# A two-layer hybrid block: transposes and some norms taken from TensorE to block transposes on VectorE and small DMAs

## The chip, the cores and the metric

The kernel runs on one core of a Trainium2 chip. A core has five engines with queues of their own: TensorE (PE in the profile; its weight loads are PEld), VectorE (DVE), ScalarE (ACT), GpSimd (POOL) and SyncE (SP), which here does nothing but issue DMAs. TensorE writes its results to PSUM, from where VectorE or ScalarE read them. The metric is device microseconds of one execution; the time of a kernel is the median of its runs.

## The reference, cut to what matters

All arithmetic is float32: 1024 tokens, width 1024, two layers. Layer 0 mixes by retention (4 heads) and by a gated delta rule (4 heads), layer 1 by a gated linear recurrence; a convolutional feed-forward follows each.

```
def _rms(x):
    return xf * lax.rsqrt(jnp.mean(xf * xf, axis=-1, keepdims=True) + EPS)

for layer in range(DEPTH):
    hn = rms_norm(h, norm_mix[layer])
    h = h + (retention_deltanet_mixer if layer % 2 == 0 else rglru_mixer)(hn, ...)
    h = h + conv_ffn(rms_norm(h, norm_ffn[layer]), ...)
return rms_norm(h, norm_final)

# retention, chunks of 128
scores = einsum('bhnid,bhnjd->bhnij', qc, kc) * dmask
intra  = einsum('bhnij,bhnjv->bhniv', scores, vc)
kv     = einsum('bhncd,bhncv->nbhdv', k_tail, vc)      # state: s = s * chunk_decay + kv_n
inter  = einsum('bhncd,nbhdv->bhncv', q_decay, s_prev)

# gated delta rule, per chunk (q and k are l2-normalised, (lmat + I) solved for u and w)
v_new = u_n - einsum('bhcd,bhdv->bhcv', w_n, s)
o = einsum('bhcd,bhdv->bhcv', qd_n, s) + einsum('bhij,bhjv->bhiv', a_n, v_new)
s = s * cd_n + einsum('bhcd,bhcv->bhdv', kt_n, v_new)
```

## The kernel before, in words

Activations are kept transposed, channels on the 128 partitions and tokens along the free axis: the residual is `H`, eight tiles of 128 x 1024. A weight matrix is streamed in quarters of 128 x 512. SP loads a quarter into `raw`, ScalarE makes its rounded part `whi` (L270), VectorE the rest `wlo` (L271), and each product is three matmuls (L328 to L330: high by high, high by low, low by high). The ring of split quarters holds six; `prefetch` keeps the loads ahead of use. A slot is one such triple over 512 tokens. `project` (L364) does one output tile of 128 channels in two halves of 512 tokens, eight slots each, and evacuates each half, multiplying by `R`, the row of inverse norms of the tokens, copied to all partitions (L388).

Small work is woven between these slots. `slot` counts them; `after(n, f)` emits `f` n slots later, and a lane is a list of generators of which one step is emitted every second slot. What is emitted is then ordered on each engine by a planner that estimates when each instruction could start; only in places marked `manual_schedule` is the written order kept.

`_mix0` is the first stage, some 470 us. In order: projections of the delta rule's k heads, q heads, gates of retention (`gate2`), v heads; meanwhile the lane `gdn` makes each chunk's matrix (`a_stage`), inverts its 32 x 32 blocks on VectorE by 31 substitution steps (L1271, L1273) by way of `l_dram` and `t_dram`, and merges them (`merge`, L1305 to L1339). Then, during the twelve projections of retention (per head q, k, v), the lane `gdn` runs the `scan` over eight chunks and the lane `ret` runs `ret_half` twice per head. Last come the gates of the delta rule and `_mix0_out`.

Things that need the other orientation go through TensorE: a transpose is a product with the identity. `scan` transposes v (L1389) and k (L1397) of a chunk, `ret_half` transposes v (L1459) and k (L1464) of four chunks, and `normalise` transposes its output eight slots later (L1366), from where ScalarE copies it and SP stores it in `y_dram`. Sums over channels, that is over partitions, are products with a column of ones: the q heads' norms (`qnorm`, L1345) and the norms of tokens (`norm_tok`, L433), whose result, inverse square roots on POOL (L438), is spread over the partitions by a product with the identity (`norm_row`, L448). `square_step` gathers the squares of eight tiles in one accumulator, but for the last tile, which is an accumulator of its own. In the scan a chunk's state product K by S (L1404), its four vector updates (L1406), L by v (L1410), the state's update (L1417, L1422) and the output (L1427, L1428) are separate lane steps. Retention's states lie in two places, used in turn, and are updated chunk by chunk between the output products (L1478, L1483).

Norms are needed in nine places of 512 or 256 tokens: the start (two halves, `norm_rest`), the two mixers' outputs (`down_pairs`, two halves each, followed by `pair_operands`, which builds the feed-forward's operands), layer 0's feed-forward output (`down_x`, two halves) and the end (`final`: 512, 256 and 256).

In the feed-forward the down product works on seven operands per set of eight pairs. `hidden` and `store_parts` store them in DRAM: operands 0, 1, 3 and 5 as two halves each (`pf_dram`, high and low), 2, 4 and 6 as one (`sf_dram`), split by ScalarE and VectorE (L840, L841) when `load_set` brings them back.

Of the kernel before, what the change touches and what calls it, by code (L numbers as in the profile page):

```python
# [19 lines left out]
P = 128  # L20
T = 1024
# [82 lines left out]
class Block:  # L104
    def __init__(self, ctx, tc, I, out, stop=None):
# [35 lines left out]
        pad(self.sm, 40, "pad3")  # L141
        self.nhalo = 0
        self.npp = 0
        self.lo_engine = nc.vector
# [42 lines left out]
    def quarter_order(self):  # L187
# [3 lines left out]
        for h in range(NH):  # L191
            o += [(("mix_in", i), 2) for i in (h, 4 + h, 8 + h)]
# [209 lines left out]
    def square_step(self, st, k, src, w=HALF):  # L402
# [14 lines left out]
        if k == KT - 1:  # L417
            st["acc"].append(sq)
        else:
            nc.vector.tensor_tensor(st["acc"][0], st["acc"][0], sq, ALU.add)  # L420

# [136 lines left out]
    def pair_operands(self, st, n, gain, gap):  # L558
# [13 lines left out]
        yield from self.norm_tok(st, wait=2)  # L572
# [3 lines left out]
        yield from range(gap)  # L576
        self.run(self.norm_row(st, apart=True))
        rows = st["rows"]
# [181 lines left out]
    def ffn(self, layer, gain):  # L760
# [3 lines left out]
        s_dram = self.tc.dram_tile([2, 4, 4, P, HALF], F32, name=f"sf_dram{layer}")  # L764
# [15 lines left out]
        place = {1: 0, 4: 1, 2: 2, 6: 3}  # L780
        whole = {0: 0, 1: 1, 3: 2, 5: 3}
        room = {}

        def store_parts(p, y, hi):
# [11 lines left out]
            def store_split(o, src, at):  # L796
                A.copy(halves(hi[:, at]), src)  # L797
                V.tensor_tensor(halves(lo[:, at]), src, f32(halves(hi[:, at])), ALU.subtract)
                for e, t in enumerate((hi, lo)):
                    nc.sync.dma_start(p_dram[c, whole[o], k % 4, e], f32(t[:, at]))  # L800
# [22 lines left out]
            store_split(5, v[:, :, 0], slice(HALF, T))  # L823

        def load_set(c, o):

            x = self.operand(o)
            if o in whole:
                for k in range(4):
                    for e in range(2):  # L830
                        nc.sync.dma_start(f32(x[:, :, 4 * e + k, :]), halves(p_dram[c, whole[o], k, e]))
# [74 lines left out]
    def final(self, ys, name):  # L906
# [13 lines left out]
        def part(t0, w, left):  # L920

            sl = slice(t0, t0 + w)
            st = {}
# [13 lines left out]
        s1 = part(512, 256, {2: [lambda: run(self.norm_tok(s0[0]))], 6: [lambda: run(self.norm_row(s0[0], 0))]})  # L937
# [14 lines left out]
    def rglru(self, gain):  # L952
# [5 lines left out]

        sm = lambda name: pool.tile([P, 8], F32, name=name)
# [12 lines left out]
        us = pool.tile([P, 8 * HALF], F32, name="us")  # L972
        xs = pool.tile([P, 4 * T], F32R, name="xs")
# [110 lines left out]
    def mix0(self, gain):  # L1084
        tc = self.tc
        self.q_dram = tc.dram_tile([NCH, P, HALF], F32, name="q_dram")
        self.v_dram = tc.dram_tile([NCH, P, HALF], F32, name="v_dram")
# [21 lines left out]
    def _mix0(self, room):  # L1109
# [89 lines left out]
        def conv_tail(kind, h, buf, dst):  # L1199
# [9 lines left out]
            return th  # L1209

# [131 lines left out]
        def qnorm(h, s):  # L1342
            p = self.pc()
            for n in range(NCH):
                PE.matmul(p[:, n:n + 1], s[:, n * P:(n + 1) * P], self.ones, start=True, stop=True)  # L1345

            V.tensor_scalar(irho[:, h * NCH:(h + 1) * NCH], p[:, 0:NCH], 4.0 * EPS, 128.0 * EPS, ALU.add, ALU.mult)

        def normalise(o, eps, ydst, i):
# [13 lines left out]
            def post():  # L1363
                p = self.pc()
                for h in range(4):
                    PE.transpose(p[:, hs(h)], on[:, hs(h)], self.ident)  # L1366
                A.copy(s, p)
                nc.sync.dma_start(ydst, ps4(s) if len(ydst.shape) == 3 else s)
            self.after(8, post)

        def scan(n):
# [4 lines left out]
            nc.sync.dma_start(v, self.v_dram[n])  # L1376
# [10 lines left out]
            pv = self.pc()  # L1387
            for h in range(NH):
                PE.transpose(pv[:, hs(h)], v[:, hs(h)], self.ident)  # L1389
# [319 lines left out]
```

## Time and profile before

| | us |
|---|---|
| median of 3 runs (2198.58 to 2200.04) | 2199.09 |
| the profiled execution | 2200.31 |
| span of its trace, first to last instruction | 2198.5 |
| PE busy | 2176.4 |
| DVE busy | 1696.0 |
| ACT busy | 1069.7 |
| POOL busy | 80.8 |

The granted TensorE clock is 0.998 over the span. Busy times of PE are of overlapping instructions, so the mean of one is longer than the time by which it moves the next; that is read from the starts in the timeline. In a row of a group the numbers after the bar are busy us, mean ns of one, and the engine's idle time before them with what ended it. In a row of waits they are us in total, times, and the longest.

### The profile page before, as it was taken

To read this page: it belongs to the slowest core of one execution; us is meant where nothing else is said; L and a number is where in the kernel's file an instruction comes from. 1 tells how busy PE (TensorE), PEld (TensorE's weight loads), DVE (VectorE), ACT (ScalarE), POOL (GpSimd) and SP (SyncE) were. 2 spreads that over 40 slices of the span, in tenths; PEclk is the share of its full clock that TensorE was granted. 3 is DMA by queue.
4 is the path that set the end of the run, shared out by engine and by line. 5 is a ranking of instruction groups with operands and counts; after the bars stand their busy time and mean duration, and the time that the engine had idled before them with its cause. 6 is when DMAs were issued, how large, how long until landed. Compare 5 with 4: busy or idle time off the path is not lost.

```text
span 2198.5 us, 29909 instructions
## 1 busy us (share of the span) xinstructions
PE 2176.4 (99%) x10844; PEld 1819.5 (83%) x10844; DVE 1696.0 (77%) x2576; ACT 1069.7 (49%) x1712; POOL 80.8 (4%) x73
## 2 busy tenths in 40 slices
PE   9999999999999999999999999999999999999998
PEld 8887888887888888887888888888888888878888
DVE  6988766446899988987865677778999889878644
ACT  5334433124565555554323476765655555544321
POOL 0100111200000000000000000000000000000001
PEclk9999999999999999999999999999999999999999
DMA  4243424125234544438546211242245445375542
GB/s 173 81 141 99 128 83 145 57 79 175 63 120 167 179 153 157 163 111 287 197 160 201 82 53 63 85 147 73 101 165 171 148 173 177 115 271 178 190 165 77
DMA packets 203300, 305.34 MB, mean 139 GB/s; under 512 B 31728, under 2 KB 91408, under 8 KB 203152
## 3 DMA queue, kind: packets, MB, share of 16 engines
q1 hardware_dynamic: 202720, 301.85, 40.7%
q8 instruction: 85, 1.39, 0.3%
q10 hardware_dynamic: 432, 1.58, 0.2%
q14 instruction: 63, 0.52, 0.1%
HBM read 212.63 MB, written 90.72 MB: 138 GB/s over the span
## 4 chain that ended last, share of the span: by engine, by line
PE 89%; DMA 4%; DVE 4%; issue 2%; ACT 1%; POOL 1%; SPq 0%; POOLq 0%; DVEq 0%; ACTq 0%
PE ps L328 27%; PE ps L330 27%; PE ps L329 27%; DMA t<-sf_dram 1%; DMA t<-y_dram 1%; PE pc L433 1%; DMA s<-pf_dram 1%; DMA h<-in_xT_dram 0%; DVE wlo L271 0%; PE pc L448 0%; DVE l L1273 0%; DVE l L1271 0%; PE pc L328 0%; PE pc L330 0%; PE pc L329 0%
## 5 line engine op out<-in xcount | busy, mean ns | idle before, releaser
L328 PE MATMUL ps<-s,whi 128*128 128x512 f32 (+1 forms) x2792 | 1091.0, 392 | 3.9 <-ACT s L840 1.8
L329 PE MATMUL ps<-s,whi 128*128 128x512 f32 (+1 forms) x2792 | 1084.5, 388 | 1.0 <-DVE s L841 0.7
L330 PE MATMUL ps<-s,wlo 128*128 128x512 f32 (+1 forms) x2792 | 1083.9, 388 | 0.0
L270 ACT CAST whi<-raw 128x512 fp32r<-128x512 f32 (+1 forms) x612 | 371.5, 613 | 659.1 <-PE ps L329 515.6
L328 PEld LDWEIGHTS ps<-s,whi 128*128 128x128 f32 x2792 | 524.9, 188 | 112.5 <-ACT s L840 3.1
L330 PEld LDWEIGHTS ps<-s,wlo 128*128 128x128 f32 x2792 | 524.7, 188 | 108.1 <-DVE wlo L271 0.3
L329 PEld LDWEIGHTS ps<-s,whi 128*128 128x128 f32 x2792 | 525.2, 188 | 107.3 <-DVE s L841 1.8
L271 DVE TENSOR_TENSOR wlo<-raw,whi 128x512 fp32r<-128x512 f32 (+1 forms) x612 | 412.9, 680 | 60.8 <-ACT whi L270 57.2
L774 DVE SCALAR_TENSOR_TENSOR t<-halo,cols,t 128x1024 f32<-128x1024 f32 x176 | 222.1, 1282 | 4.8 <-ACT t L772 3.5
L747 DVE TENSOR_TENSOR halo<-ps,kept 128x512 f32<-128x512 f32 (+1 forms) x138 | 92.2, 668 | 75.5 <-PE ps L330 74.2
L757 DVE TENSOR_TENSOR h<-ps,h 128x512 f32<-128x512 f32 x112 | 77.4, 691 | 82.2 <-PE ps L330 81.9
L772 ACT ACTIVATE t<-halo,cols 128x1024 f32<-128x1024 f32 x88 | 109.7, 1246 | 16.9 <-DVE halo L747 11.6
L742 ACT COPY kept<-ps 128x512 f32<-128x512 f32 (+1 forms) x138 | 77.0, 558 | 13.3 <-PE ps L330 11.2
L498 DVE TENSOR_TENSOR h<-ps,h 128x512 f32<-128x512 f32 (+1 forms) x72 | 45.3, 631 | 43.3 <-PE ps L330 43.3
L438 POOL TENSOR_TENSOR rtok<-rtok,npow 128x4 f32<-128x4 f32 (+1 forms) x11 | 11.2, 1016 | 1722.3 <-DVE rtok L437 1668.7
L857 DVE TENSOR_TENSOR t<-t 128x1024 f32<-128x1024 f32 x44 | 53.7, 1221 | 0.0
L797 ACT CAST t<-t 128x512 fp32r<-128x512 f32 x64 | 38.1, 620 | 32.0 <-DVE t L857 30.7
L852 ACT ACTIVATE t<-t 128x1024 f32<-128x1024 f32 x44 | 46.8, 1063 | 10.1 <-DVE t L774 10.0
L416 ACT ACTIVATE t<-h 128x512 f32<-128x512 f32 (+1 forms) x49 | 27.2, 562 | 46.3 <-DVE h L498 41.5
L840 ACT CAST s<-t 128x512 fp32r<-128x512 f32 x48 | 29.5, 621 | 38.4 <-DMA t<-sf_dram 34.0
L328 PE MATMUL ps<-s,s 128*128 128x256 f32 (+1 forms) x144 | 46.2, 321 | 0.0
L329 PE MATMUL ps<-s,s 128*128 128x256 f32 (+1 forms) x144 | 45.8, 318 | 0.0
(293 smaller groups left out, 2074.5 us busy)
## 6 DMA issues: line engine op xcount, KB each, us to landing
raw<-in_ffn_up_dram SPq DMA_DIRECT2D x176, 256.0 KB, 2.7
s<-pf_dram SPq DMA_DIRECT2D x128, 256.0 KB, 5.3
pf_dram<-t SPq DMA_DIRECT2D x64, 256.0 KB, 2.6
pf_dram<-lo SPq DMA_DIRECT2D x64, 256.0 KB, 2.5
sf_dram<-t SPq DMA_DIRECT2D x64, 256.0 KB, 2.2
t<-sf_dram SPq DMA_DIRECT2D x64, 256.0 KB, 5.0
raw<-in_ffn_w_dram SPq DMA_DIRECT2D x64, 256.0 KB, 2.9
raw<-in_mix_in_dram SPq DMA_DIRECT2D x62, 256.0 KB, 2.9
```

Source lines behind the costliest of these rows:

```text
L270: self.nc.scalar.copy(hi[:, 0:w], raw[:, 0:w])
L271: eng.tensor_tensor(lo[:, 0:w], raw[:, 0:w], f32(hi[:, 0:w]), ALU.subtract)
L328: mm(ps, whi, xhi, start=start, stop=False)
L329: mm(ps, whi, xlo, start=False, stop=False)
L330: mm(ps, wlo, xhi, start=False, stop=stop)
L742: A.copy(kept[o], ps)
L747: V.tensor_tensor(dst(i, j), v(ps), v(kept[k]), ALU.add)
L757: V.tensor_tensor(h(*to[o]), ps.rearrange("p (h c) -> p h c", c=256), h(*to[o]), ALU.add)
L772: A.activation(t, buf[:, 2:2 + T], AF.Identity, scale=w(0), bias=self.col(f"ffn_cb{layer}", tile_i))
L774: V.scalar_tensor_tensor(t, buf[:, 2 + j:2 + j + T], w(j), t, ALU.mult, ALU.add)
L852: A.activation(tg, tg, AF.Silu)
L857: V.tensor_tensor(tg, tg, tv, ALU.mult)
```

## The change: block transposes and DRAM in place of TensorE

VectorE's block transpose turns each 32 x 32 block of a tile in its place; the blocks are then put in their transposed places by DMAs, four per tile, in runs of 32 values (128 bytes), on the way to DRAM.

- `store_t` does this for the delta rule's k (`kt_dram`, from where `scan` now loads a chunk) and v (`v_dram`, now tokens first), and for retention's v and k (`rt_dram`), half by half. `ret_load` brings retention's back for a whole head. Retention's projections come in the order v, k, q.
- `normalise` transposes by blocks at once and stores in 4 DMAs (scan) or 16 (retention).
- `qnorm` transposes the squares by blocks, reduces each block's rows on VectorE, sends the partial sums through `qq_dram` and reduces again.
- `norm_beside` does the same for one half's norm in four places (first half of both `down_pairs`, of `down_x` and of `final`): sums to DRAM, back as four tokens per partition, inverse root on POOL, to DRAM, back on all partitions in `R`. With `whole`, the last tile's squares are added to the one accumulator.
- In `scan` the product K by S stands in the first step, beside K by q, and a step is gone; in `ret_half` all four states of a half are made before the outputs, in four places.
- In the feed-forward's first set operand 5 is stored once and split at the load, like 2, 4 and 6.

```diff
     def square_step(self, st, k, src, w=HALF):
...
-        if k == KT - 1:
+        if k == KT - 1 and not st.get("whole"):
             st["acc"].append(sq)
         else:
             nc.vector.tensor_tensor(st["acc"][0], st["acc"][0], sq, ALU.add)
...
+    def block_sums(self, out, src, room):
+        self.nc.vector.transpose(room, src)
+        self.nc.vector.tensor_reduce(out, room.rearrange("p (b j) -> p b j", j=32), AX.X, ALU.add)
+
+    def norm_beside(self, st, n):
...
+        self.block_sums(b, st["acc"][0], st["free"])
+        for a in range(4):
+            nc.sync.dma_start(sums[a].rearrange("(b i) -> i b", i=32), b[32 * a:32 * a + 32, :])
+        x = small("ntok")
+        nc.sync.dma_start(x.rearrange("p (a c) -> p a c", a=4), sums.rearrange("a (p c) -> p a c", c=4))
...
+        V.tensor_reduce(r, x.rearrange("p (a c) -> p c a", a=4), AX.X, ALU.add)
+        V.tensor_scalar(r, r, 1.0 / D, EPS, ALU.mult, ALU.add)
+        nc.gpsimd.tensor_tensor(r, r, self.npow[:, 0:4], ALU.pow)
+        nc.sync.dma_start(row.rearrange("(p c) -> p c", c=4), r)
+        nc.sync.dma_start(self.R[:, n * HALF:(n + 1) * HALF], row.partition_broadcast(P))
+        self.has_row[n] = True
...
     def down_x(self, ys, name, gain):
...
+            st["whole"] = True
...
-                self.steps((9, 7)[n], self.norm_rest(st, n, 3))
+                if n == 0:
+                    self.norm_beside(st, n)
+                else:
+                    self.steps(8, self.norm_rest(st, n, 3))
...
     def down_pairs(self, ys, name, gain):
...
+            st["whole"] = n == 0
             self.square_step(st, m, h)
             if m == KT - 1:
+                if n == 0:
+                    self.norm_beside(st, n)
                 self.build[n] = self.pair_operands(st, n, gain, 4)
-                self.steps(3, self.build[n])
+                self.steps((16, 3)[n], self.build[n])
...
-        whole = {0: 0, 1: 1, 3: 2, 5: 3}
+        whole = [{0: 0, 1: 1, 3: 2}, {0: 0, 1: 1, 3: 2, 5: 3}]
...
+        def store_t(dst, src, room):
+            V.transpose(room, src)
+            for a in range(4):
+                bs = slice(a * 32, (a + 1) * 32)
+                nc.sync.dma_start(dst[:, bs].rearrange("(b i) j -> i b j", i=32),
+                                  room[bs, :].rearrange("p (b j) -> p b j", j=32))
...
-        def qnorm(h, s):
-            p = self.pc()
-            for n in range(NCH):
-                PE.matmul(p[:, n:n + 1], s[:, n * P:(n + 1) * P], self.ones, start=True, stop=True)
...
+        def qnorm(h, s, room):
+            V.transpose(room, s)
+            V.tensor_reduce(q32, room.rearrange("p (b j) -> p b j", j=32), AX.X, ALU.add)
+            d = self.qq_dram[h]
+            for a in range(4):
+                nc.sync.dma_start(d[a].rearrange("(b i) -> i b", i=32), q32[a * 32:(a + 1) * 32, :])
+            for a in range(4):
+                nc.sync.dma_start(qx[:, a * NCH:(a + 1) * NCH], d[a].rearrange("(n p) -> p n", p=P))
+            rho = irho[:, h * NCH:(h + 1) * NCH]
+            V.tensor_reduce(rho, qx.rearrange("p (a n) -> p n a", a=4), AX.X, ALU.add)
...
         def normalise(o, eps, ydst, i):
...
-            def post():
-                p = self.pc()
-                for h in range(4):
-                    PE.transpose(p[:, hs(h)], on[:, hs(h)], self.ident)
-                A.copy(s, p)
-                nc.sync.dma_start(ydst, ps4(s) if len(ydst.shape) == 3 else s)
-            self.after(8, post)
+            V.transpose(s, on)
+            for a in range(4):
+                bs = slice(a * 32, (a + 1) * 32)
+                for d, c in ydst(a):
+                    nc.sync.dma_start(d, s[bs, c].rearrange("p (m j) -> p m j", j=32))
...
         def scan(n):
...
-            nc.sync.dma_start(v, self.v_dram[n])
+            nc.sync.dma_start(v, self.v_dram[cs])
+            if n < NCH - 1:
+                kt = tmp2("kt")
+                nc.sync.dma_start(kt, self.kt_dram[cs])
+                V.tensor_tensor(ps4(kt), ps4(kt), bc_last(cn(ekt), P), ALU.mult)
+            V.tensor_tensor(ps4(v), ps4(v), bc_last(cn(cv), P), ALU.mult)
...
-            pv = self.pc()
-            for h in range(NH):
-                PE.transpose(pv[:, hs(h)], v[:, hs(h)], self.ident)
-            V.tensor_tensor(ps4(v), ps4(pv), bc_last(cn(cv), P), ALU.mult)
+            s0, s1 = S[n % 2], S[(n + 1) % 2]
+            if n > 0:
+                ks = self.pc()
+                for h in range(NH):
+                    PE.matmul(ks[:, hs(h)], K[h][:, cs], s0[:, hs(h)], start=True, stop=True)
+                for h in range(NH):
+                    V.scalar_tensor_tensor(v[:, hs(h)], ks[:, hs(h)], col(ck, h, n), v[:, hs(h)], ALU.mult, ALU.add)
...
+        def ret_load(h):
+            for i in range(2):
+                for e in range(2):
+                    nc.sync.dma_start(ps4(rt[i][e]),
+                                      self.rt_dram[e, h, i * HALF:(i + 1) * HALF].rearrange("(c p) d -> p c d", p=P))
+                nc.scalar.activation(rt[i][1], rt[i][1], AF.Copy, scale=ktail[:, h:h + 1])
...
-            self.after(28, lambda h=h, q2=q2: qnorm(h, q2))
+            qnorm(h, q2, blocks())
+            store_t(self.kt_dram[:, hs(h)], K[h], blocks())
...
-            q = rot_head(h)
-            k = rot_head(4 + h)
-            unit = self.unit("mix_in", 8 + h)
-            v = self.t()
-            self.project(unit, self.evac_r(v))
-            ret += [ret_half(h, i, q, k, v) for i in range(2)]
+            def evac(n, sl, ps):
+                v = half()
+                V.tensor_tensor(v, ps, self.R[:, sl], ALU.mult)
+                store_t(self.rt_dram[0, h, sl], v, half())
+            self.project(self.unit("mix_in", 8 + h), evac)
+            k = rot_head(4 + h, self.rt_dram[1, h])
+            q = rot_head(h)
+            ret_load(h)
+            ret += [ret_half(h, i, q, k) for i in range(2)]
```

More of the change, by code (lines that the diff above doesn't have):

```diff
@@ L570, in normal @@
             V.tensor_tensor(dst, dst, bc_mid(rows[j], 4), ALU.mult)
-        yield from self.norm_tok(st, wait=2)
+        if n == 0:
+            rows = self.R[:, 0:256], self.R[:, 256:HALF]
+        else:
+            yield from self.norm_tok(st, wait=2)
         scaled(b11, 0, 0)
@@ L575, in pair_operands @@
         scaled(b12, 0, 1)
-        yield from range(gap)
-        self.run(self.norm_row(st, apart=True))
-        rows = st["rows"]
+        if n == 1:
+            yield from range(gap)
+            self.run(self.norm_row(st, apart=True))
+            rows = st["rows"]
         place = lambda o: [self.operand(o)[:, n, e:e + 4, :] for e in (0, 4)]
@@ L1483, in ret_half @@
                     V.scalar_tensor_tensor(s1, s0, RET_CD[h], kv[:, hs(c)], ALU.mult, ALU.add)
[L1484 removed]
+            yield from range(3)
+            o = self.pc()
+            for c in range(4):
+                n = n0 + c
+                if n > 0:
+                    PE.matmul(o[:, hs(c)], qd[:, hs(c)], rs[n % 4], start=True, stop=False)
+                PE.matmul(o[:, hs(c)], sc[:, hs(c)], vt[:, hs(c)], start=n == 0, stop=True)
+            y = self.y_dram[h].rearrange("(b i) t -> i b t", i=32)
+            normalise(o, None, lambda a: [(y[:, :, (n0 + c) * P + a * 32:(n0 + c) * P + (a + 1) * 32], hs(c))
+                                          for c in range(4)], 1)
         def together(*gens):
@@ L1494, in together @@
                 yield from range(2)
+        blocks = lambda: f32(self.parts.tile([P, T], F32R, tag="lo", name="lo"))
+        half = lambda: self.kept.tile([P, HALF], F32, tag="kept", name="kept")
         gdn = self.lane("gdn", 2, 0)
```

107 lines of the change are left out of this document (52 added, 55 removed).

## The prediction

> **What bounds the kernel now.** I read the page's busy times and chain of waits first, then TensorE's waits, then its groups by line and shape, then the timeline around the groups that the change removes.
>
> ```profile
> span 2198.5 us, 29909 instructions
> PE 2176.4 (99%) x10844; PEld 1819.5 (83%) x10844; DVE 1696.0 (77%) x2576; ACT 1069.7 (49%) x1712; POOL 80.8 (4%) x73
> PE 89%; DMA 4%; DVE 4%; issue 2%; ACT 1%; POOL 1%; SPq 0%; POOLq 0%; DVEq 0%; ACTq 0%
> ```
>
> ```profile
> PE pc L1478 <- DVE l L1483: 2.2, 4, 0.6
> PE ps L328 <- ACT s L840: 1.8, 3, 1.0
> ```
>
> TensorE (PE) has no gap worth the name: 2176.4 of 2198.5 us, 89% of the chain, and its two longest waits in the whole span total 2.2 and 1.8 us. So each microsecond of TensorE's queue that goes shortens the program, as long as no other engine becomes late. VectorE (DVE) is the one to watch, at 77% on average.
>
> **What is removed from TensorE.** These are its groups by line and shape; the last two columns are busy us and mean ns of one, then idle time.
>
> ```profile
> L433 PE MATMUL pc<-ones,t 128*128 128x1 f32 x96 | 11.4, 245 | 0.7 <-ACT t L416 0.7
> L448 PE MATMUL pc<-ident,rtok 128*128 128x128 f32 x80 | 10.9, 277 | 1.3 <-POOL rtok L438 1.3
> L1366 PE MATMUL pc<-ident,l 128*128 128x128 f32 x64 | 9.6, 272 | 0.0
> L433 PE MATMUL pc<-ones,halo 128*128 128x1 f32 x64 | 7.6, 240 | 0.0
> L1345 PE MATMUL pc<-ones,l 128*128 128x1 f32 x64 | 7.4, 245 | 0.0
> L1464 PE MATMUL pc<-ident,t 128*128 128x128 f32 x32 | 4.8, 273 | 0.0
> L1389 PE MATMUL pc<-ident,l 128*128 128x128 f32 x32 | 4.8, 273 | 0.0
> L1459 PE MATMUL pc<-ident,t 128*128 128x128 f32 x32 | 4.8, 272 | 0.0
> L1397 PE MATMUL pc<-ident,h 128*128 128x128 f32 x28 | 4.2, 272 | 0.0
> ```
>
> A mean of 272 ns is a latency; instructions overlap. What one takes of the queue is read from start to start in TensorE's timeline (start, us, line):
>
> ```profile
> 100.45 1.84 PE L1345 MATMUL pc<-ones,l 128*128 128x1 f32 x16
> 102.15 0.49 PE L328 MATMUL ps<-s,whi 128*128 128x512 f32 x1
> 102.47 0.40 PE L329 MATMUL ps<-s,whi 128*128 128x512 f32 x1
> ...
> 274.73 0.39 PE L330 MATMUL ps<-s,wlo 128*128 128x512 f32 x1
> 274.96 0.60 PE L1397 MATMUL pc<-ident,h 128*128 128x128 f32 x4
> 275.40 1.06 PE L1404 MATMUL pc<-l,h 128*128 128x128 f32 x8
> ...
> 277.68 0.60 PE L1366 MATMUL pc<-ident,l 128*128 128x128 f32 x4
> 278.12 1.06 PE L1410 MATMUL pc<-l,h 128*128 128x128 f32 x8
> ```
>
> Four transposes take 274.96 to 275.40, or 277.68 to 278.12: 0.44 us, 0.11 each. Sixteen passes against the column of ones take 1.70 us, and the matmul behind them starts its successor after 0.32 us where 0.23 is usual (274.73 to 274.96): 1.79, 0.11 each.
>
> Transposes removed: L1366, L1389, L1397, L1459, L1464, 64+32+28+32+32 = 188, all of them; at 0.11, 20.7 us. The q norms, L1345: 64 x 0.112 = 7.2 us. Norms: an fp32 product counts twice in these rows, so a half of 512 tokens costs 16 of L433 (two accumulators of four chunks) and 8 of L448. Four halves lose both: 4 x 24 = 96. Where "whole" merges the accumulators and the norm stays on TensorE, 8 go in each of three halves (both of the start, the second after layer 0's feed-forward) and 4 in the final quarter: 28. Together 124 x 0.113 = 14.0 us. **TensorE's queue: -41.9 us.** No matmul is added.
>
> The Trainium skill, "VectorE: DVE Perf Modes", section "Rules for kernel authors", says the opposite of this change: a 128x128 transpose belongs on TensorE where PSUM can take it. By that rule the moves would cost and not gain; the rows above say that TensorE is the only full engine, so I let the rule lose as long as VectorE has room.
>
> **What VectorE gets.** No row shows a block transpose. The nearest:
>
> ```profile
> L1277 DVE COPY l<-l 128x1024 f32<-128x1024 f32 x1 | 1.1, 1112 | 0.0
> L1236 DVE TENSOR_REDUCE l<-l 128x4 f32<-128x512 f32 x8 | 5.4, 680 | 0.0
> L1406 DVE SCALAR_TENSOR_TENSOR l<-pc,l 128x128 f32<-128x128 f32 x28 | 8.0, 345 | 0.5 <-PE pc L1404 0.5
> ```
>
> A strided copy of 1024 columns takes 1.11 us; the dearest full-height rate is 345 ns for 128, which is 2.76 us for 1024. I take 1.2 us (0.69 for 512), next to the copy, and keep 1.1 to 2.8.
>
> ```profile
> 88.00:147.00 59.00, 59.00 (x330) 50.95 (x329) 49.37 (x123) 25.52 (x53) 9.37 (x4) 1.00 0.45 126
> 147.00:190.00 43.00, 43.00 (x191) 35.61 (x190) 40.58 (x89) 10.01 (x13) 0.00 (x0) 1.00 0.37 130
> ...
> 240.00:330.00 90.00, 87.53 (x589) 77.28 (x589) 62.09 (x124) 33.11 (x81) 19.84 (x16) 1.00 0.32 93
> 330.00:470.00 140.00, 138.62 (x805) 120.04 (x804) 70.93 (x135) 35.78 (x68) 30.43 (x24) 1.00 0.28 92
> 547.00:592.00 45.00, 45.00 (x212) 37.66 (x211) 37.77 (x50) 26.81 (x47) 1.01 (x1) 1.00 0.23 70
> 1020.00:1045.00 25.00, 23.31 (x94) 16.63 (x93) 15.37 (x24) 11.65 (x18) 0.00 (x0) 1.00 0.93 333
> ```
>
> (Stretch, length, then busy us of PE, PEld, DVE, ACT, POOL; clock; DMA share; GB/s.)
>
> *q and gate stretch, 88 to 190.* Per q head: transpose 1.2, reduction over 1024 about 1.2, the small reduction 0.2, K's transpose 1.2: 3.8 us, 15 us for four (28 at the dear end). VectorE idles 59 - 49.4 = 9.6 us there and 2.4 us in the next stretch, while TensorE now arrives 7.2 us sooner. So VectorE falls some 15 - 9.6 + 7.2 = 12.8 us further behind. What hides that is the lead of the weight splits:
>
> ```profile
> 139.44 0.69 DVE L271 TENSOR_TENSOR wlo<-raw,whi 128x512 fp32r<-128x512 f32 x1
> ...
> 152.45 0.69 DVE L388 TENSOR_TENSOR t<-ps,R 128x512 f32<-128x512 f32 x1 [0.31 <-PE ps L330]
> ```
>
> The evacuation at 152.45 ends the third gate's first half of 24 matmuls at 0.23 (5.5 us), so its second quarter is first used at about 149.7; that quarter's split ended at 140.1: 9.6 us of lead, the smallest I found. 12.8 - 9.6 leaves 3.2 us; the substitution steps (L1271, L1273) can also be put off, since projections can run before the merges. I take **+3.5**, bounds 0 and 16 (12.8 more at the dear end, no lead gained elsewhere).
>
> *Scan and retention, 240 to 470.* Added: 8 + 8 + 16 transposes of 512, 22 us, against 28 + 69 us idle: hidden. But transposes also gave cover: between the state product L1404 and L1410, which waits for four L1406 (1.4 us), stood two slots of projection and L1366's 0.44. Without it up to 0.44 in each of seven chunks shows: **+3**, bounds 0 and 7. The chunk also gives up one lane step; the next chunk's values must land before their multiplication, where they had to land before a transpose, at the same place. Retention's values and keys now come back from DRAM; these loads follow the q projection (11 us) that is put behind them, so I cost them at nothing; uncovered, 2.2 us in each of four heads, 9. Four state places take the state update off the output products' path: nothing on TensorE, below nothing by at most the 2.2 us of L1478's wait. ScalarE loses copies.
>
> *Norms beside.* Two 128x512 passes and small ones, about 2.2 us of VectorE per half, and a chain of four DMA hops (below). The second half's products last 64 slots of 0.69 us, 44 us, and VectorE idles 7 us in 547 to 592: nothing; uncovered, 3 us each. "whole" adds one 0.69 us addition ahead of three norms still on the path to their evacuations: **+0.5**, 0 to 2.
>
> **What the queues get.** SP issues about 290 DMAs more in the first stage and a few for the norms:
>
> ```profile
> q_dram<-t SPq DMA_DIRECT2D x4, 512.0 KB, 3.3
> l_dram<-h SPq DMA_DIRECT2D x32, 16.0 KB, 1.5
> l<-gc_dram SPq DMA_DIRECT2D x16, 256.0 KB, 4.5
> gc_dram<-l SPq DMA_DIRECT2D x1, 16.0 KB, 2.8
> ```
>
> ```profile
> 99.13 1.76 SPq L1246 DMA_DIRECT2D l_dram<-h  x4
> ```
>
> 0.44 us an issue: 128 us over 400, of which no more than 7 us in a block (16 stores of one retention half). Loads of weights behind such a block lose less than their 9.6 us lead. A quarter of a head's transpose is 1024 packets of 128 bytes; q's store is 1024 of 512 bytes and lands in 3.3 us, 128 packets of 128 bytes in 1.5: so 1.5 to 3.3 us, and nothing on the path. The norms' chain is 4 issues + 1.5 to 2.8, load 2 to 4.5, POOL 1.0, store 2, broadcast 4.5: 13 to 17 us, inside 44.
>
> *Feed-forward's operand 5.* In the first set it is stored once instead of as two halves, and split at the load: 4 x 256 KB come in instead of 8. In 1020 to 1045 the DMA engines are 93% busy at 333 GB/s and TensorE idles 1.7 us; 1 MB is 3.1 us of that. Four splits (0.69 DVE) fit in VectorE's 9.6 idle. **-2** for both layers, bounds -3.4 and +3.
>
> **Sum.** The profiled execution took 2200.3 us (span 2198.5), 1.2 above the median of the runs, 2199.09. 2200.3 - 41.9 + 3.5 + 3 + 0.5 - 2 = 2163.4; for the median, **2162**.
>
> **Rivals.** *All of it and more:* no stall, DMA relief, scan waits gone: 2199 - 41.9 - 3.4 = 2154. For it: 9.6 us lead, idle VectorE after 190. Against: 94% VectorE from 147 to 190. 0.13.
>
> *VectorE bounds the first stage:* transposes at the dear end, 16 lost there, 7 in the scan: 2199 - 42 + 23 = 2180. 0.14.
>
> *Slower: VectorE stands still for DRAM.* The q norms' second reduction sits on VectorE behind eight issues (3.5 us), a store (2.8) and a load (4.5): 10.8 us. If it stands in the queue where it is written, ahead of K's transpose, four heads lose 43 us. With 12.8 behind and 9.6 of lead, TensorE loses 46, plus 3 in the scan: 2199 - 42 + 49 = 2206. It decides from about 39 us lost, near 9 us a head. Against it: VectorE's order isn't the written one:
>
> ```profile
> 101.84 0.17 DVE L1256 SCALAR_TENSOR_TENSOR l<-l 128x8 f32<-128x8 f32 x1 [1.44 <-POOL l L1254]
> ...
> 104.22 0.16 DVE L1255 SCALAR_TENSOR_TENSOR l<-l 128x8 f32<-128x8 f32 x1
> ```
>
> L1256 is written after L1255; a planner moved it forward by its own estimate of POOL, and was 1.44 us too hopeful. It will put the reduction later, and err by a few us, not by ten. The same side is reached if packets are far slower than 3.3 us a thousand. 0.08. The Trainium skill's "The three transpose paths" (same page) warns that a plain DMA copy that transposes by strides is 19 times slower than the hardware transpose. Here the strides are outside runs of 128 bytes, which the traced 1.5 us for such runs shows to be no such trap.
>
> *The removal is hidden anyway,* TensorE waiting elsewhere for as long: 2199. The two wait rows are against. 0.03.
>
> **Chances.** Forecast 0.62 (its own range 2155 to 2172), the others as given. A measurement of this kernel tells 0.2% (4.4 us) from no change: faster 0.89, within 0.04, slower 0.07. Range 2151 to 2188: it leaves out the slower and hidden cases and the ends of two others.
>
> **What would show it.** No L1366, L1389, L1397, L1459, L1464, L1345 groups; L433 at 68, L448 at 48; TensorE still 99% busy. Wrong steps would show as TensorE waiting for wlo between 110 and 180 us (lead), for L1406's counterpart (cover), or VectorE idle behind the q norms' load. Transposes of 1024 far from 1.2 us move the first term. A time over 2190 says that VectorE, not TensorE, sets the first stage.

## The result and the profile after

The changed kernel takes 2350.4 us (median of 4 runs, 2346.7 to 2351.5) against 2199.6 of the kernel before on the same chip: ratio 1.068, 95% interval 1.067 to 1.070. It is 151 us slower; 2162 was forecast. The profiled execution took 2351.0 us. Line numbers (L) of a run are those of its own kernel. The page of this run, with the busy times and two rows of the 40 slices (TensorE's share in tenths, the granted clock):

```profile
span 2349.3 us, 29614 instructions
PE 2191.3 (93%) x10468; PEld 1819.3 (77%) x10468; DVE 1742.1 (74%) x2648; ACT 1053.1 (45%) x1686; POOL 81.5 (3%) x73
...
PE   9967995579898999999999999999899999999997
...
PEclk9988997789999999999999999999999999999998
```

What was to be taken off TensorE is off: 10844 - 10468 = 376 instructions, as counted. But its share fell from 99% to 93%, and the holes lie in the first dozen slices, the first stage, where the granted clock falls too (0.963 over the span, 0.998 before). VectorE is at 74% as against 77%: it is not full, it waits as well. TensorE's waits, which were 2.2 and 1.8 us at the longest sums before:

```profile
PE pc L1470 <- DVE l L1464: 30.2, 7, 10.4
PE ps L329 <- ACT whi L271: 24.3, 7, 10.0
PE ps L329 <- DVE t L389: 21.7, 2, 12.2
PE pc L1290 <- DVE h L1302: 12.7, 2, 10.3
PE pc L1457 <- DMA l<-q_dram: 11.8, 2, 9.2
```

L1470 and L1457 are products of the scan, L389 (the evacuation of a projection) and L1302 belong to the q stretch, and L271 is a weight's split that waits for its load. The block transposes themselves cost what was forecast (1.2 us for 1024 columns, 0.69 for 512):

```profile
L1405 DVE STREAM_TRANSPOSE lo<-l 128x1024 f32<-128x1024 f32 x4 | 5.0, 1240 | 1.7 <-DMA kt_dram<-lo 1.7
L1431 DVE STREAM_TRANSPOSE l<-l 128x512 f32<-128x512 f32 x16 | 11.3, 709 | 0.3
```

What cost more stands in three views: the DMA issues (number, size of one, median us from issue to landing), VectorE's timeline (start, us, line; in brackets the idle time ahead and what ended it) and SP's timeline (start, us, issues):

```profile
qq_dram<-l SPq DMA_DIRECT2D x16, 4.0 KB, 12.9
l<-qq_dram SPq DMA_DIRECT2D x16, 4.0 KB, 3.4
```

```profile
99.32 0.69 DVE L1295 TENSOR_TENSOR l<-pc,ident 128x512 f32<-128x512 f32 x1
108.84 0.21 DVE L1413 TENSOR_REDUCE l<-l 128x8 f32<-128x32 f32 x1 [8.83 <-DMA l<-qq_dram]
```

```profile
89.41 2.16 SPq L1409 DMA_DIRECT2D qq_dram<-l  x4
91.67 0.51 SPq L1268 DMA_DIRECT2D kt_dram<-lo  x1
97.93 8.58 SPq L1411 DMA_DIRECT2D l<-qq_dram  x4
106.55 2.23 SPq L1268 DMA_DIRECT2D kt_dram<-lo  x3
...
111.03 8.68 SPq L261 DMA_DIRECT2D raw<-in_mix_in_dram  x3
```

The first q head: SP issues the store of the sums at 89.4; each of the four loads has to wait for its store, so the last leaves only at 106.5. VectorE stands 8.83 us for it, with everything that is queued behind, and 34.3 us over the four heads. K's stores and a weight's load stand behind it on SP.

The Trainium skill, "DMA: Bandwidth & Descriptors", section "Rules for kernel authors", says that a strided last dimension becomes one descriptor for each element. The trace agrees: for the 32 transfers of 1024 elements, e16 (below) moves 33 thousand packets more than the kernel before. A store of 4 KB as 1024 elements of 4 bytes took 12.9 us.

### The profile page after: what moved, and what is told of

Its sections match the earlier page's. It is cut to its first block, busy times and chain, and to the rows that moved or that the text cites. A ratio compares the mean times of both kernels' runs of the same rounds, so it can differ in the third digit from the quotient of the medians.

```text
span 2349.3 us, 29614 instructions
## 1 busy us (share of the span) xinstructions
PE 2191.3 (93%) x10468; PEld 1819.3 (77%) x10468; DVE 1742.1 (74%) x2648; ACT 1053.1 (45%) x1686; POOL 81.5 (3%) x73
## 5 line engine op out<-in xcount | busy, mean ns | idle before, releaser
L271 ACT CAST whi<-raw 128x512 fp32r<-128x512 f32 (+1 forms) x612 | 369.4, 612 | 645.8 <-PE ps L330 461.6
L898 ACT ACTIVATE t<-t 128x1024 f32<-128x1024 f32 x44 | 46.8, 1063 | 11.5 <-DVE t L816 11.5
L1420 ACT ACTIVATE l<-pc 128x512 f32<-128x512 f32 x16 | 9.6, 597 | 88.0 <-PE pc L1488 31.1
L886 ACT CAST s<-t 128x512 fp32r<-128x512 f32 x56 | 34.2, 620 | 30.4 <-DMA t<-sf_dram 26.2
L329 PE MATMUL ps<-s,s 128*128 128x256 f32 (+1 forms) x144 | 46.7, 324 | 0.0
```

Of the source, the lines that this page charges most:

```text
L271: self.nc.scalar.copy(hi[:, 0:w], raw[:, 0:w])
L329: mm(ps, whi, xhi, start=start, stop=False)
L898: A.activation(tg, tg, AF.Silu)
```

## The experiments

The expectations name five theories. A: a store or a reduction that waits stands at the head of SP's or VectorE's queue. B: VectorE has too much work. C: many small packets make the transfers long. D: the planner's order puts the projections ahead of the merges, so that the scan is left without them. E: SP is filled by the issues themselves. Ratios are to the kernel before, with a 95% interval; 1% is 22 us. e1, e2 and e3 have two runs each, the others four to twelve.

### The q norms

**e1_qnorm_te** puts the q norms back on TensorE and leaves the rest changed.

```diff
-            qnorm(h, q2, blocks())
+            self.after(28, lambda h=h, q2=q2: qnorm(h, q2))   # 8 products with the ones
```

> The changed kernel with the q norms back on TensorE (products with the column of ones, 28 slots later); all else changed. Changed kernel 2350, before 2200. Theory A (the q norms' way through DRAM holds the in-order queues: VectorE stands 34 us in all for the load, and SP's loads of weights and of the gates' row stand behind it; the substitution starts 72 us later and ends 100 us later): nearly all of those 100 us come back, less 7 us of TensorE: 2250 to 2275. Theory B (VectorE is simply full; the q norms are 10 of the 24 us it was given there): about 10 us come back, 2335 to 2345. Theory C (the 16 DMA engines are short of packets per second; q norms bring 33 of the 144 thousand packets added): a fifth of the loss, about 2320.

Measured: 1.0459 (1.0435 to 1.0484), some 49 us less, half of what A expected. **e16_qnorm_alone** is the reverse: the kernel before with the q norms alone changed.

> The kernel before with only the q norms changed, written as in the changed kernel (4-byte elements, the second reduction where it is written). Theory D: 206 of 228 weight products stay in the scan, so it loses little there; 7.2 us come off TensorE: 2195 to 2210. Theory A (VectorE stands for four round trips, some 11 us each): 2225 to 2245, as its removal from the changed kernel gave 47.

Measured: 1.0228 (1.0209 to 1.0247), 2251.1 us, which is above A's range too. The loss is the part's own. TensorE's waits in e16, and the two largest of VectorE from 80 to 520 us:

```profile
PE ps L328 <- DVE halo L388: 13.4, 1, 13.4
PE pc L1231 <- DVE h L1243: 11.1, 3, 10.4
PE ps L328 <- DVE t L388: 11.1, 1, 11.1
```

```profile
DVE l L1232 <- DMA l<-gc_dram: 22.0, 3, 11.0
DVE l L1354 <- DMA l<-qq_dram: 21.7, 4, 9.9
```

Evacuations of projections (L388) stand on VectorE behind instructions that wait for a load, and TensorE waits for them. Only half of VectorE's waiting is for the sums (L1354). The other half is for the gates' row (L1232), although its loads were not changed: those that SP issued right behind the sums' stores landed late, the slowest after 14.7 us, where 6.1 was the longest in the kernel before. So the 4-byte elements also hold up the transfers that are issued behind them.

**e6_qnorm_later** emits loads and second reduction 28 slots later in the changed kernel; **e7_qnorm_128** turns the sums by a 32x32 transpose on either side, so that each row is 128 contiguous bytes; the store's part of the edit:

```diff
-            for a in range(4):
-                nc.sync.dma_start(d[a].rearrange("(b i) -> i b", i=32), q32[a * 32:(a + 1) * 32, :])
+            V.transpose(qt, q32)
+            nc.sync.dma_start(d.rearrange("a (b i) -> (a b) i", i=32), qt)
```

> The changed kernel with one edit: the q norms' loads from DRAM and their second reduction are emitted 28 slots later, where the kernel before had its products for them; the four stores of 4-byte elements stay where they are. Theory A (VectorE stands for the round trip, and SP for the store ahead of the load): most of the 47 us that came back when the q norms went to TensorE: 2303 to 2318. Theory B: VectorE's work is the same, 2345 to 2351. Theory C (packets): their number is the same, 2345 to 2351, as the stores take 12.9 us whoever waits for them.

> The changed kernel with one edit: the q norms' sums pass a 32x32 block transpose on each side of DRAM, so that the store is 128 packets of 128 bytes instead of 4096 of 4 bytes, and the load as well; the second reduction stays where it is written. Theory C (the number of packets makes the round trip long): the store takes some 1.5 us instead of 12.9, about 11 us less in each of four heads: 2305 to 2318. Theory A (VectorE stands for any round trip): the trip still has two hops and five issues, some 8 us of the 20, so about half comes back: 2320 to 2335. Theory B: two small transposes more on VectorE, 2350 to 2354.

Measured: e6 1.0534 (1.0515 to 1.0553), e7 1.0475 (1.0459 to 1.0490): of the 2.25% that e1 gave back, e6 gives 1.5 (2322 us, 4 above A's range) and e7 2.1 (2308 us, as C expected). In e7 the same 16 KB take:

```profile
qq_dram<-l SPq DMA_DIRECT2D x4, 16.0 KB, 1.4
l<-qq_dram SPq DMA_DIRECT2D x16, 4.0 KB, 1.7
```

So C's cause makes the trip long (11.5 us less in the store alone), and A's is how it costs: either a short trip or a later reader removes most of it. Why the later reader gives less shows in e6's trace: the elements are still stored, K's transposed stores behind them take up to 13.1 us to land (4.7 in e7), and VectorE stands 12.1 us for one of these.

### The outputs

**e2_out_te** transposes the outputs of scan and retention on TensorE again, with one store each, 8 slots later; **e3_qnorm_out_te** does this and e1.

> The changed kernel with the outputs of scan and retention transposed on TensorE and stored eight slots later, as before; all else changed. Theory A (SP's queue: the stores of a chunk wait for VectorE's transpose, and the next chunk's loads and the weights stand behind them; from the first scan to the end of the gates 41 us are lost): 25 to 40 us come back there, plus 7 of TensorE: 2315 to 2330. Theory B (full VectorE): it is busy about half of that stretch, so little comes back, 2345 to 2355. Theory C (packets): 33 of 144 thousand, about 2320; the trace then has to show the DMA engines near full in the scan, where the changed kernel shows them under 0.6.

> Both put back: q norms and outputs on TensorE as before; the transposes of k and v, the four norms and operand 5 stay changed. Theory A: both gains add, 2215 to 2240. Theory B: VectorE keeps 21 us of the transposes, 2320 or more. Theory C: half of the packets are left, 2275.

Measured: e2 1.0361 (1.0334 to 1.0388), 71 us less, twice what any theory had expected (35 at most); e3 1.0198 (1.0175 to 1.0221), 107 us less, 14 short of the sum of the two. Three runs take e2 apart. **e5_out_later** keeps VectorE's transposes and all 160 stores, but 8 slots later. **e12_out_pool** keeps their place and issues them on POOL's queue. **e17_out_te_160** is e2 with 4 or 16 stores for one. The edits, shortened:

```diff
-            V.transpose(s, on)                     # e5: all of it inside post()
+            self.after(8, post)
```

```diff
-                    nc.sync.dma_start(d, s[bs, c]...)     # e12
+                    nc.gpsimd.dma_start(d, s[bs, c]...)
```

```diff
-                nc.sync.dma_start(ydst, s)          # e17
+                for a in range(4):                  # and c in range(4) for retention
+                    nc.sync.dma_start(ydst[bs, hs(c)], s[bs, hs(c)])
```

> The changed kernel with one edit: the block transpose on VectorE and the four or sixteen stores at the end of normalise are emitted 8 slots later, where the kernel before had its transposes and its store. Transposes and packets stay as changed. Theory A (a store that waits for VectorE stands on SP ahead of the next chunk's loads): most of the 69 us that came back when these transposes went to TensorE and their stores came later: 2280 to 2295. Theory B (VectorE has too much work): no transpose leaves VectorE, 2340 to 2350. Theory C (128-byte packets take the DMA engines' time): packets unchanged, 2340 to 2350.

> The changed kernel with one edit: the 160 stores of the scan's and retention's outputs are issued from POOL's queue instead of SP's. Theory A (these stores stand on SP ahead of the next chunk's loads and of the weights' loads): most of the 69 us that came back with the outputs on TensorE: 2280 to 2300. Theory D (the scan stands alone because its projections are spent): 52 weight products in the scan as against 44, so next to nothing in the scan, and only the weights' loads after it gain: 2325 to 2345.

> The kernel with its outputs transposed on TensorE again (2282), but each output stored in as many pieces as in the changed kernel, 4 from a chunk of the scan and 16 from a half of retention, 144 issues more on SP. Theory E (the issues themselves fill SP, 0.44 to 0.67 us each, 63 to 96 us in the 200 us in which it also loads the chunks and the weights): 2315 to 2337. Theory B (the transposes on VectorE and their place in its order cost it): 2280 to 2292.

Measured: e5 1.0605 (1.0586 to 1.0623), e12 1.0623 (1.0607 to 1.0638), e17 1.0543 (1.0528 to 1.0559). From the changed kernel to e5 (later) 0.8%, from e5 to e17 (TensorE for VectorE) 0.6%, from e17 to e2 (16 stores for 160) 1.8%, 40 us. So A was wrong on e5: more than half of what e2 gave back is the number of issues, as E expected. SP in e17 (raw are loads of weights):

```profile
409.43 0.49 SPq L261 DMA_DIRECT2D raw<-in_mix_in_dram  x1
...
421.19 7.53 SPq L1442 DMA_DIRECT2D y_dram<-l  x16
431.25 1.77 SPq L1439 DMA_DIRECT2D y_dram<-l  x4
...
439.62 8.18 SPq L1442 DMA_DIRECT2D y_dram<-l  x16
...
451.91 0.97 SPq L261 DMA_DIRECT2D raw<-in_mix_in_dram  x2
```

7.53 us for 16 issues, 0.47 each; 144 more are 68 us of SP. The weights pay for it: no load of a quarter leaves between 409 and 452 us, and from 430 to 500 us six leave, where e2 issues fourteen. From 440 to 460 us TensorE is busy 9.7 of 20 us, in e2 18.7. The scan itself is hardly slower: its loads of v span 100 us in e17 and 98 in e2.

e12 came out in D's range (2337 us), but it tells less than it was meant to, as POOL's own work then stood behind the stores (one of TensorE's waits in e12, 330 to 600 us):

```profile
PE pc L1527 <- POOL t L1503: 20.2, 3, 9.1
```

The Trainium skill, "DMA: Bandwidth & Descriptors", section "Issuing engines are not separate DMA queues", calls the issuing engine's time usually small beside the transfer. Here a store of 16 KB landed in 1.5 us and took 0.47 of SP, and the issues decided.

### K, v and retention's k and v

**e8_kv_alone** is the kernel before with these alone. **e9_blocks_unused** keeps scan and retention as before and adds VectorE's transposes of K and v with their stores; nobody reads them.

```diff
+            store_t(self.kt_dram[:, hs(h)], K[h], blocks())     # e9, behind each q head
...
+            store_t(self.vt_dram[:, hs(h)], v, blocks())        # and behind each v head
```

> The kernel before with one part of the change alone: K, v and retention's k and v are transposed in blocks on VectorE and go by DRAM, retention has four state places and its q projection last; q norms, norms of the halves, outputs of the scan and of retention and the feed-forward's operand 5 are as before. By difference of two runs (q norms and outputs undone, less the norms alone: 2245.7 - 2220.7) it should take 25 us more than before, 2225; by closure of the parts (2350 less 47, 69 and 17) 18 more, 2217. Theory A: the loss lies in the scan, 300 to 400 us, where v and K are needed within a chunk of being loaded. Theory B: the loss lies between 90 and 190 us, where VectorE is 94% busy. My forecast before the result put this part at 9.5 us faster than before, 2190.

> The kernel before, which does its whole work as before, with VectorE's block transposes of K and of v and their stores to DRAM added in the q and value stretches; what they store is not used. Theory D (the planner's order: VectorE's added work makes the substitution late, so projections are put ahead of the merges and the scan is left without them): in the order that was written out for TensorE 52 weight products are left in the scan instead of 228; 176 x 0.23 = 40 us of TensorE's work that ran beside the scan runs before it, and the scan's chain then stands alone: 2225 to 2240, as slow as the kernel that also uses them. Theory A (the scan's own loads and its changed steps are what costs): the scan is the old one, 2199 to 2206.

Measured: e8 1.0123 (1.0102 to 1.0145), e9 1.0174 (1.0161 to 1.0187). The added work costs as much when nobody uses it (the 124 transposes that e8 takes off, 13.6 us, stay on TensorE in e9), so most of it isn't the scan's own changes. TensorE's weight products within the scan, by line, in the kernel before and in the changed one:

```profile
L328 PE MATMUL ps<-s,whi 128*128 128x512 f32 x76 | 32.7, 430 | 0.0
L330 PE MATMUL ps<-s,wlo 128*128 128x512 f32 x77 | 30.3, 394 | 0.0
L329 PE MATMUL ps<-s,whi 128*128 128x512 f32 x76 | 29.9, 394 | 0.0
```

```profile
L329 PE MATMUL ps<-s,whi 128*128 128x512 f32 x15 | 7.0, 467 | 4.9 <-DVE kept L1665 3.7 <-ACT whi L271 1.2
L331 PE MATMUL ps<-s,wlo 128*128 128x512 f32 x15 | 6.6, 451 | 0.0
L330 PE MATMUL ps<-s,whi 128*128 128x512 f32 x15 | 6.6, 438 | 0.0
```

229 stood there, 45 are left (51 in e8, 52 in e9). The others ran earlier, while substitution and merges were late. One chunk of the scan follows another by some 13 us, and now little stands beside it. TensorE in e8:

```profile
312.92 0.79 PE L1417 MATMUL pc<-l,h 128*128 128x128 f32 x2 [3.74 <-DVE l L1411]
...
318.39 0.63 PE L1434 MATMUL pc<-l 128*128 128x128 f32 x2
318.82 0.64 PE L1435 MATMUL pc<-l 128*128 128x128 f32 x2
...
328.03 0.49 PE L1417 MATMUL pc<-l,h 128*128 128x128 f32 x2 [4.33 <-DVE l L1411]
...
332.42 0.39 PE L1434 MATMUL pc<-l 128*128 128x128 f32 x2
332.65 0.39 PE L1435 MATMUL pc<-l 128*128 128x128 f32 x2
```

Two products take 0.43 us at 318 and 0.23 at 332. The granted clock in this trace is 0.50 from 312 to 320 us, behind the first wait, and from 329 to 330, behind the second, and 1.00 again from 332: after a wait the clock is at half for a while. The Trainium skill, "TensorE: Matmul & The Clock Gate", section "What's actually happening", gives the half clock after an idle window of some 3.4 us; waits of 3.7 and 4.3 us here agree with it. But a wait of 3.0 us in the same trace (at 304.6 us) was followed by a clock of 0.50 as well, so a shorter one is enough here.

Is it the missing projections (D)? **e10_k_late** writes K's transposes behind the v heads. **e15_kv_each_slot** is e8 with the chain's steps emitted in every slot, **e14_before_each_slot** its control, **e13_lane_each_slot** the same number in the changed kernel. In e14 and e15 the merges then begin before the last q norms are summed, and they share room with the squares: those norms are sums over other contents, by the same instructions.

```diff
-        gdn = self.lane("gdn", 2, 0)
+        gdn = self.lane("gdn", 1, 0)
```

> The kernel with K, v and retention's k and v by DRAM alone, with K's four block transposes and stores written after the value heads instead of one behind each query head. The number of transposes is the same. Theory D: 99 weight products are left in the scan, between 51 (2229) and 228; about a quarter of the lost cover comes back: 2212 to 2222. Theory A: the scan's loads and steps are unchanged, 2226 to 2232.

> The changed kernel with one number edited: the chain of a stage, substitution, merges and scan's wait emits a step in every slot, not in every second. All transposes, stores and loads stay. Theory D (the scan is left without projections): in the order that is written out for TensorE 282 weight products stand in the scan instead of 44, 238 x 0.23 = 55 us of cover back, and the chain starts earlier: 2250 to 2295. Theory A (stores and round trips stand in the queues of SP and VectorE whatever the order): 2335 to 2352.

> Control: the kernel before with the same number edited. 228 weight products stand in the scan, as before. Both theories: 2195 to 2206, no difference that matters.

> K, v and retention's k and v by DRAM alone (2229), with the same number edited. Theory D: 210 weight products in the scan instead of 51, so most of the 36 us between 2229 and 2193 (the kernel before less 92 transposes of 0.11) come back: 2190 to 2208. Theory A: 2222 to 2232.

Measured: e10 1.0171 (1.0158 to 1.0184), e13 1.0578 (1.0557 to 1.0598), e14 1.0042 (1.0026 to 1.0059), e15 1.0123 (1.0104 to 1.0143). D misses three times: e10 has more weight products in the scan than e8 (99) and is slower, e15 has nearly all of them (211) and is no faster, and e13, with 283, stays 32 us above D's range. (The 92 transposes in e15's expectation are 124.) Against its control, which is itself 0.4% slower, e15 loses 0.8% instead of 1.2, and e13 is 1.1% better than the changed kernel. So the order is some part of it, and the larger part is not. What VectorE and SP wait for in e15, and TensorE's largest wait in e9, where nothing of the scan was changed (us in all, times, longest):

```profile
DVE l L1394 <- DMA l<-v_dram: 7.4, 1, 7.4
```

```profile
SPq L1221 <- DVE kept L1218: 38.1, 8, 7.8
SPq L1221 <- DVE lo L1218: 32.5, 4, 11.7
```

```profile
PE pc L1400 <- DMA l<-v_dram: 11.1, 4, 5.1
```

SP stands for VectorE's block transposes (L1218), and a chunk's v comes 7.4 us late in e15 and up to 5.1 late in e9. That fits A; no run takes it away alone, and the share of each cause stays open.

**e11_ret_alone** takes retention's part alone, with four state places.

> The kernel before with only retention's k and v by block transposes and DRAM, four state places and its q projection last; scan, norms and outputs as before. It takes 64 transposes off TensorE, 64 x 0.11 = 7 us. Theory D: the order keeps 228 weight products in the scan, so the gain stays: 2190 to 2195. Theory A (a round trip by DRAM stands ahead of something on SP): 8 us or more lost in four heads, 2199 to 2210.

Measured: 1.0019 (1.0010 to 1.0027). Here all weight products stay in the scan (230), and still the 7 us are not gained. In their place stand waits of TensorE, of which the two largest are:

```profile
PE pc L1379 <- DVE l L1374: 4.0, 4, 1.5
PE pc L1430 <- ACT l L1425: 3.3, 1, 3.3
```

### The norms beside, and a version without the waits

**e4_norms_alone** is the kernel before with the norms by DRAM and the single accumulators.

> The kernel before with nothing but the norms changed: four halves' norms by VectorE and DRAM, one accumulator where the change has it. By my prediction: 14 us of TensorE gone and nothing given back, 2186. Theory A (the row of inverse norms comes later than the queue counts on; in the changed kernel VectorE waits 24 us for the sums, 9 for the row, and TensorE 6 to 9 us at each of three places): 2200 to 2212, slower or the same.

Measured: 1.0088 (1.0067 to 1.0110), 2220.6 us, above both ranges. VectorE in e4 around a half's end, then the stretch behind it (length, busy PE, PEld, DVE, ACT, POOL, clock):

```profile
562.20 0.18 DVE L446 TENSOR_REDUCE rtok<-ntok 128x4 f32<-128x16 f32 x1 [5.41 <-DMA ntok<-nsum_dram]
...
569.62 3.50 DVE L608 TENSOR_TENSOR t<-t,R 128x1024 f32<-128x1024 f32 x3 [4.39 <-DMA R<-nrow_dram]
```

```profile
580.00:600.00 20.00, 15.98 (x72) 12.62 (x70) 20.00 (x28) 15.74 (x30) 0.00 (x0) 0.91 0.08 27
```

VectorE stands 9.8 us in all for two hops, is then 100% busy for the next 20 us, and TensorE loses 4 of them.

**e18_late_128** keeps what neither waits nor moves the order much: one accumulator at the start, operand 5 stored once, q norms by 128 bytes with store and reduction 10 and 28 slots later.

> The kernel before with three parts that neither wait in a queue nor move much in the order: one accumulator in the two halves at the start (16 passes off TensorE, 1.8 us), the feed-forward's operand 5 stored once (-2 by my forecast), and the q norms by VectorE and DRAM (7.2 us off TensorE), but as 128-byte packets, their store 10 and their load and second reduction 28 slots later. 224 of 228 weight products stay in the scan. By the sum 2199.1 - 11 = 2188; theory A and D alike: 2186 to 2194. If VectorE's 2.6 us a head (10 us for four) already show in the q stretch, 94% full behind it: 2195 to 2205.

Measured: 1.0024 (1.0014 to 1.0035). VectorE no longer waits for the q norms' data, TensorE has 9 us less to do, and the kernel is 5 us slower:

```profile
120.00:140.00 20.00, 14.08 (x53) 11.19 (x52) 17.07 (x40) 8.02 (x17) 2.60 (x1) 0.83 0.37 97
140.00:160.00 20.00, 17.93 (x80) 14.53 (x79) 18.46 (x41) 5.89 (x7) 2.72 (x1) 1.00 0.53 153
```

(Same columns as above.) TensorE idles 8 us in 120 to 160, with VectorE 85 to 92% busy, and a slice of it runs at a clock of 0.83. That fits theory B, with four heads of 2.6 us; VectorE is not full there, so where the planner put the new instructions in its queue can have a share, which no run separates. No version found here beats the kernel before.

## Why the prediction was wrong

*TensorE's queue, -41.9.* Right in number (376 instructions) and worth little here, since TensorE was no longer what set the end of the first stage.

*The q norms.* This is the step that failed first: the wait for the round trip was put at nothing. The slower rival priced a head at 10.8 us, with a store of 2.8, and the forecast then cost it at nothing, because the planner "will put the reduction later, and err by a few us". In e16 four heads lose 2.28% = 50 us plus the 7.2 that were taken off TensorE, 14.3 us a head. The store is 12.9 us: the row that I took for it (16 KB in one issue, 2.8 us) moves rows, not elements. The words "no such trap" held for the runs of 128 bytes that they were about; the q norms' sums go in 4-byte elements. And the planner left the reduction where VectorE waits 8.8 us for it, 34.3 over four heads: it did not err by a few us. The rival had the right place and mechanism, at a chance of 0.08, though not the late landing of what is issued behind the stores.

*VectorE in the q and gate stretch, +3.5.* The transposes' prices were right. The lead of 9.6 us was the wrong cover: e18 shows some 18 us lost (9 and 4 taken off, 5 slower) for 10 us of VectorE's work, above my +3.5 and above the bound of 16. e9 shows that 10 us more with 32 stores, for K and v, lose 38. The transposes of v, 4.9 us, stood in no term of the sum.

*What the queues get.* "No more than 7 us in a block", and loads "lose less than their lead": the block was right (7.53), and so was an issue's price. But the 128 us that the sum gave were set against 400 us and put at nothing. 144 issues of 0.47 us are 68 us of SP in the 200 us in which it must also bring each chunk's q, v and K and the weights, and SP stands for the outputs before it can store them. e17 against e2 prices the number alone at 40 us; I had nothing.

*Scan and retention, +3.* "Hidden" was worked out from VectorE's idle sum of 97 us. The scan's chunk is a chain of 13 us; what counted was where in the chain each wait fell and, for some part, whether projections stood beside it. e8 measures +27 where I had 13.6 us off TensorE, +3 here and a share of the +3.5.

*Norms beside, nothing.* The chain of 13 to 17 us was put inside 44. But VectorE's queue stands for two of the hops (5.41 and 4.39 in e4), and the work behind them comes late in one piece: e4 loses 0.88% = 19 us though 14.0 are off TensorE, so 33 for four halves, where "uncovered" was priced at 3 each.

*Operand 5, -2.* In e18's trace each feed-forward ends 2.0 us less late against the kernel before than it began, so -4 for both: right in sign, twice my size and a little past the bound of -3.4.

The parts alone add to 2.28 + 0.88 + 1.23 = 4.4%; with the 3.2% that the outputs gave back in e2, 7.6, less the 0.2 of operand 5, 7.4 against 6.8 measured. e3, which has only the norms, K and v and operand 5 left, measures 2.0 where these add to 1.9. So no large part is missing, and the overlap lies between the q norms and the outputs.

## What to carry to other kernels

Before moving work off the full engine, list for each new transfer what stands behind it on its issuing queue and behind its reader, and price it by packets and by issues, not by bytes: 4 KB in elements of 4 bytes were 12.9 us and made a load issued behind them take 14.7, and 144 issues cost 40. An engine's idle sum in a stage is not room for a chain; on an engine 85 to 94% busy, 10 us more work cost 18 (e18), and 38 with its stores (e9). Where a round trip can't be avoided, turn the data so that a packet is a whole row, and emit the reader later than the trip.

## What the runs showed that was not expected

The planner's order is part of the cost: 10 us more on VectorE moved some 180 weight products ahead of the scan (e9). Small packets hold up other transfers: in e16 half of VectorE's waits for loads in the q stretch were for a row that the change did not touch. And the granted clock can fall while TensorE is busy. In e14, with merges closer together and fewer weight products between them:

```profile
160.00:200.00 40.00, 40.00 (x296) 32.21 (x296) 32.24 (x67) 14.27 (x24) 0.00 (x0) 0.98 0.29 88
200.00:240.00 40.00, 39.53 (x465) 29.22 (x462) 20.20 (x44) 18.43 (x39) 0.00 (x0) 0.81 0.32 81
```

The second stretch is 99% busy at a clock of 0.81. What these small products lack for the full clock no run here shows.
